# A tuned eight-core decoder kernel: the list order refined in a second pass, idle TensorE of the opening filled, and the last tile scaled by two engines

## The chip, the cores and the metric

The kernel runs on all 8 cores of one Trainium2 chip, one sample of the batch on each core. The metric is the time of the slowest core in microseconds (us). Profiles are taken on all cores of one execution; cores 0 to 3 are one die, 4 to 7 the other. A program on all cores has a second, slower state in some of its executions, in which cores of one die (or of both) run at a lower granted clock; times below are of fast runs unless it is said otherwise.

The engines are named TensorE (PE in the profile, its weight loads PEld), VectorE (DVE), ScalarE (ACT), GpSimd (POOL) and SyncE (SP, which only issues transfers here).

## The reference

A trunk of two layers, each with three sub-layers, on `x` of 8 samples x 2048 tokens x 1024 features:

```python
def modulate(x, g, mod):
    shift, scale, gate = jnp.split(mod, 3, axis=-1)
    h = rmsnorm(x, g) * (1.0 + scale[:, None, :]) + shift[:, None, :]
    return h, gate[:, None, :]

def swiglu(h, w_in, w_out):
    g, u = jnp.split(h @ w_in, 2, axis=-1)
    return (jax.nn.silu(g) * u) @ w_out

def reference(x, c, ...):
    c_act = jax.nn.silu(c)
    for l in range(DEPTH):                              # 2
        mod = c_act @ w_mod[l] + b_mod[l]               # (B, 9*D): one row of w_mod per number
        mod_f1, mod_mx, mod_f2 = jnp.split(mod, N_SUB, axis=-1)
        h, gate = modulate(x, norm_g[l, 0], mod_f1)
        x = x + 0.5 * gate * swiglu(h, w_ffn_in[l, 0], w_ffn_out[l, 0])
        h, gate = modulate(x, norm_g[l, 1], mod_mx)
        x = x + gate * mixer(h)                         # even l and odd l differ
        h, gate = modulate(x, norm_g[l, 2], mod_f2)
        x = x + 0.5 * gate * swiglu(h, w_ffn_in[l, 1], w_ffn_out[l, 1])
    return rmsnorm(x, final_g)
```

Two things matter here. Before the first matmul of the trunk can run, `h` needs the mean square of `x` and the numbers `shift` and `scale`, which are dot products of `c_act` with rows of `w_mod`. And all later sub-layers need further such rows, in the background.

## The kernel before

`x` lies in SBUF as 8 chunks of features (128 partitions) by 4 tiles of 512 tokens. The program is first recorded operation by operation by a greedy scheduler with a cost model, and then listed again: `relist` computes for each operation a due date backward from the greedy start times, and simulates the engines, each taking the ready operation with the earliest due date. The order that comes out is what each engine executes; at run time every engine follows its list strictly in order.

```python
    def relist(self, free=("dve", "act")):
        ...
        for o in ops:
            cost.append(o.end - o.start if o.semkey is None else o.issue)   # (two branches in the original)
            due.append(o.start + (0.0 if o.eng == "pe" else 8.0))
        ...                                   # due dates pulled forward along the dependencies
        while events:
            ...                               # each free engine takes the ready operation due first
    ...
    Sd.relist(("dve", "act", "pe"))           # once
```

Background work (row dots, squares) is recorded only while VectorE has little queued:

```python
    def slack():
        return Sd.tl["dve"].busy_after(Sd.tl["pe"].tail() - 0.5) < SLACK      # SLACK = 3

    def row_dma(q, where=None):               # load a row of wmod, 512 KB
        ...
        add("sp", I("dma_start", out=ap, in_=wmod_d[q]), writes=keys, cost=0.06, dma=dk, nbytes=128 * 4096)

    def row_dot(q):                           # its dot product, on VectorE
        ...
        stt(ap, ap, 1.0, CB[:], ALU.mult, ALU.mult, keys + ["CB"], [("MOD", 0, q)], n=1024, accum_out=MODT[:, q:q + 1])
```

In the opening 16 rows are needed. Four of them have their dot products on TensorE, as eight one-column fp32 matmuls each (the trace shows them as 16 instructions), the rest on VectorE. Fillers, matmuls whose result nobody reads, keep TensorE from idling; each has a fixed earliest time:

```python
    on_pe = (10, 12, 14, 15)
    ...
            if n in on_pe:
                for kc in range(NC):
                    add("pe", I("matmul", PS[b][:, 0:1], ap[:, kc * 128:(kc + 1) * 128], CT[:, kc:kc + 1], ...), ...)
            else:
                stt(ap, ap, 1.0, CB[:], ALU.mult, ALU.mult, keys + ["CB"], [("MOD", 0, q)], n=1024, accum_out=M)
    ...
    for n in range(WARM):                     # WARM = 36
        op = mm(PS[5][:], ONES[:], SQ[:, n % NSQ, :], True, True, [("SQ", n % NSQ), "ONES"], [("ps", 5)])
        op.after = 28.0 + n * 0.6
```

The last tile is scaled by VectorE in eight multiplies, stored two chunks at a time:

```python
                    rstd([3], True)           # 1/rms of the last tile: two activations, result in SBUF
                    for c in range(NC):
                        final_chunk(3, c)     # VectorE: X = X * g * rstd; a store after every second chunk
```

## Time and profile before

| | before |
|---|---|
| time, median of the first 3 runs | 1938.27 us (1936.89 to 1973.97; the longest is a slow run) |
| span of the profiled run, by core | 1927.7 to 1933.5 us |
| start of the 100th trunk matmul, mean of the cores | 86.6 us |
| from there to the last update of `x`, mean (least disturbed core) | 1831.7 us (1829.2) |
| from the last update to the end, mean | 12.1 us |

The last three rows cut the span at work, not at times, so that kernels can be compared although everything in them shifts: the **opening** up to the 100th matmul that reads a weight slot, the **body**, and the **tail**. They are worked out from each core's instruction records, and their sum is the core's span. The mean over the cores is of use for the opening and the tail. In the body the least disturbed core shows what the program itself takes. The lines of the profile that carry the argument are in the prediction.

### The profile page before, as it was taken

How to read it: one execution, taken by the hardware profiler on the slowest of the kernel's cores; microseconds unless marked ns; L12 is line 12 of the kernel's file. 1: busy time of each engine (PE TensorE's matmuls, PEld its weight loads, DVE VectorE, ACT ScalarE, POOL GpSimd, SP SyncE). 2: the span in 40 equal slices, each digit the busy share in tenths (PEclk: the TensorE clock that was granted, in tenths of full speed). 3: DMA queues.
4: the chain of work that ended last, by engine and by line, in shares of the span. 5: the costliest groups of instructions: out<-in, count | busy, mean ns of one | idle time of the engine just before them, and what ended most of it. 6: DMA issues, size and time to landing. Idle time of an engine off the chain costs nothing.

```text
span 1933.5 us, 25425 instructions; the slowest of 8 cores (1927.7 to 1933.5 us)
## 1 busy us (share of the span) xinstructions
PE 1880.4 (97%) x8706; PEld 853.4 (44%) x8706; DVE 1694.7 (88%) x3256; ACT 1030.3 (53%) x1738; POOL 174.6 (9%) x330
## 2 busy tenths in 40 slices
PE   3999999999999999999999999999999999999997
PEld 1544444444444444444444444444444444444443
DVE  4897999999988999999988888888998899898865
ACT  3444754456454564555456554654556655664343
POOL 0000000001212000000000000000000000000000
PEclk9899999999999999999999999999999999999999
DMA  9799568797676686867664554555453545445752
GB/s 278 147 174 218 92 119 184 177 190 155 169 177 157 143 190 148 168 137 158 148 119 81 89 87 83 89 96 88 77 88 66 87 77 94 78 74 87 175 86 95
DMA packets 67517, 248.72 MB, mean 129 GB/s; under 512 B 7616, under 2 KB 7744, under 8 KB 67136
## 3 DMA queue, kind: packets, MB, share of 16 engines
q0 software_dynamic: 42192, 153.64, 47.6%
q1 hardware_dynamic: 25200, 93.45, 15.1%
q8 instruction: 74, 1.21, 0.2%
q14 instruction: 51, 0.42, 0.1%
HBM read 392.29 MB, written 8.39 MB: 207 GB/s over the span
## 4 chain that ended last, share of the span: by engine, by line
PE 88%; DMA 4%; DVE 3%; ACT 2%; SPq 1%; issue 1%; POOL 0%; DVEq 0%
PE ps L465 88%; DMA WMOD<-wmod 3%; DMA SLOTS<-win 1%; SPq L465 1%; DVE WMOD L465 1%; DVE SLOTS L465 1%; DVE ACTB L465 1%; DVE TP L465 1%; DVE X L465 0%; ACT ps L465 0%; ACT PMH L465 0%; DVE ps L465 0%; ACT ACTB L465 0%; ACT TP L465 0%; ACT L465 0%
## 5 line engine op out<-in xcount | busy, mean ns | idle before, releaser
L465 PE MATMUL ps<-H,SLOTS 128*128 128x512 f16 x5440 | 1199.7, 379 | 9.3 <-ACT ps L465 3.3
L465 PEld LDWEIGHTS ps<-H,SLOTS 128*128 128x128 f16 x5440 | 530.1, 98 | 657.5 <-issue 28.3
L465 ACT ACTIVATE ps<-ps 128x512 f32<-128x512 f32 x684 | 397.0, 582 | 567.8 <-PE ps L465 529.1
L465 PE MATMUL ps<-ACTB,SLOTS 128*128 128x512 f16 x2780 | 613.8, 379 | 0.1
L465 PEld LDWEIGHTS ps<-ACTB,SLOTS 128*128 128x128 f16 x2780 | 271.8, 98 | 328.4 <-issue 1.4
L465 DVE TENSOR_TENSOR SLOTS<-SLOTS 128x512 f16<-128x512 f16 x996 | 395.0, 417 | 17.0 <-DMA SLOTS<-win 10.3
L465 DVE SCALAR_TENSOR_TENSOR X<-ps,GH,X 128x512 f32<-128x512 f32 x424 | 307.7, 743 | 38.0 <-PE ps L465 34.8
L465 ACT ACTIVATE TP<-ps 128x512 f32<-128x512 f32 x400 | 237.9, 595 | 129.2 <-PE ps L465 126.1
L465 DVE TENSOR_TENSOR ACTB<-TP,ps 128x512 f16<-128x512 f32 x368 | 248.6, 683 | 36.2 <-PE ps L465 22.7
L465 ACT ACTIVATE SQ<-X 128x512 bf16<-128x512 f32 x224 | 131.0, 622 | 111.3 <-DVE X L465 53.6
L465 POOL DMA_DIRECT2D SLOTS<-win x176 | 93.0, 530 | 1032.5 <-PE ps L465 957.8
L465 DVE TENSOR_TENSOR TP<-ps,TP 128x512 f32<-128x512 f32 x176 | 121.0, 687 | 52.4 <-ACT ps L465 50.8
L465 DVE SCALAR_TENSOR_TENSOR WMOD<-WMOD,CB 128x1024 f32<-128x1024 f32 x130 | 157.7, 1216 | 7.0 <-DMA WMOD<-wmod 6.9
L465 DVE TENSOR_TENSOR TP<-X,RS 128x512 f32<-128x512 f32 x192 | 128.8, 686 | 8.1 <-ACT ACTB L465 5.0
L465 DVE TENSOR_TENSOR ps<-ps,TP 128x512 f32<-128x512 f32 x176 | 122.3, 695 | 12.6 <-PE ps L465 10.9
L465 DVE TENSOR_TENSOR ACTB<-ACTB 128x1024 f16<-128x1024 f16 (+1 forms) x188 | 104.3, 565 | 1.4
L465 POOL DMA_DIRECT2D SLOTS<-wout x88 | 46.4, 528 | 502.2 <-PE ps L465 502.2
L465 PE MATMUL ps<-SQ,ONES 128*128 128x512 bf16 x166 | 56.6, 427 | 29.4 <-ACT SQ L465 24.3
L465 ACT ACTIVATE H<-TP,MODT,AS 128x512 f16<-128x512 f32 x81 | 62.5, 805 | 20.3 <-DVE TP L465 13.6
L465 ACT ACTIVATE PMH<-TP,MODT,AS 128x512 f16<-128x512 f32 x60 | 47.5, 805 | 18.9 <-DVE TP L465 18.7
L465 ACT ACTIVATE ACTB<-TP,MODT,AS 128x512 f16<-128x512 f32 x51 | 40.6, 808 | 13.2 <-PE ps L465 7.0
L465 DVE TENSOR_TENSOR SQ<-SQ 128x1024 bf16<-128x1024 bf16 (+1 forms) x56 | 36.2, 647 | 10.5 <-ACT SQ L465 10.1
(74 smaller groups left out, 539.1 us busy)
## 6 DMA issues: line engine op xcount, KB each, us to landing
SLOTS<-win POOLq DMA_DIRECT2D x176, 512.0 KB, 5.7
WMOD<-wmod SPq DMA_DIRECT2D x131, 512.0 KB, 5.9
SLOTS<-wout POOLq DMA_DIRECT2D x88, 512.0 KB, 5.4
SLOTS<-wab POOLq DMA_DIRECT2D x28, 512.0 KB, 8.7
outT<-X SPq DMA_DIRECT2D x16, 512.0 KB, 3.3
ACTB<-wmod SPq DMA_DIRECT2D x13, 512.0 KB, 28.6
X<-xT SPq DMA_DIRECT2D x2, 2048.0 KB, 22.1
X<-xT SPq DMA_DIRECT2D x8, 512.0 KB, 9.7
```

Source lines behind the costliest of these rows:

```text
L465: return lambda E: getattr(E, name)(*a, **k)
```

## The change

The intent, in three parts:

1. **Fillers wherever TensorE is idle.** Up to 150 instead of 36, without fixed times; the listing places one whenever TensorE has nothing else and cuts them off when the 21st TensorE operation after the opening is reached. The modelled transfer rate of the opening falls from 295 to 285 GB/s.
2. **Two passes of listing.** The second takes the start times of the first as its due dates. With it the slack for background work goes from 3 to 2.5.
3. **The last tile on two engines.** Five of its chunks on VectorE, reading the root from PSUM, three on GpSimd after ScalarE, stored from two queues; the squares of its last two chunks are no longer added in pairs.

```diff
-WARM = 36
+WARM = 150
+PASSES = 2
...
-            due.append(o.start + (0.0 if o.eng == "pe" else 8.0))
+            due.append(1e9 if o.filler else o.start + (0.0 if o.eng == "pe" else 8.0))
...
+        stop = [o.idx for o in ops if o.eng == "pe" and self.fill_to is not None and o.idx >= self.fill_to][20:21]
...
+                if x in stop:
+                    filling = False
+                if o.filler:
+                    o.filler = 1 if filling else 2
+                    cost[x] = o.issue if filling else 0.0
...
-    SLACK = 3
+    SLACK = 2.5
...
+    def final_part(t, a, b, eng):
+        for c in range(a, b):
+            if eng == "dve":
+                stt(Xv(c, t), Xv(c, t), SM[:, SM_FG + c:SM_FG + c + 1], PS[0][:], ALU.mult, ALU.mult, ...)
+            else:
+                act(Xv(c, t), Xv(c, t), AF.Copy, ..., scale=SM[:, SM_FG + c:SM_FG + c + 1])
+                add("pool", I("tensor_tensor", out=Xv(c, t), in0=Xv(c, t), in1=RS[:, t % 2, :], op=ALU.mult), ...)
+        add("sp" if eng == "dve" else "act", I("dma_start", ...), ...)
...
-    Sd.BW = 295e3
+    Sd.BW = 285e3
...
-        op = mm(PS[5][:], ONES[:], SQ[:, n % NSQ, :], True, True, ...)
-        op.after = 28.0 + n * 0.6
+        op = add("pe", I("matmul", PS[5][:], ONES[:], SQ[:, n % NSQ, :], ...), ..., cost=0.0)
+        op.issue, op.filler = c_pe(TT), 1
...
-                    rstd([3], True)
-                    for c in range(NC):
-                        final_chunk(3, c)
+                    rstd([3], True, load=(0.0, 0.0), bank=0)
+                    act(RS[:, 1, :], PS[0][:], AF.Copy, [("ps", 0)], [("RS", 1)])
+                    for a, b, eng in ((3, 5, "dve"), (0, 2, "pool"), (5, 7, "dve"), (2, 3, "pool"), (7, 8, "dve")):
+                        final_part(3, a, b, eng)
...
-    Sd.relist(("dve", "act", "pe"))
+    for _ in range(PASSES):
+        Sd.relist(("dve", "act", "pe"))
```

More of the change, by code (lines that the diff above doesn't have):

```diff
@@ L41 @@
     __slots__ = ("idx", "eng", "fn", "deps", "semkey", "start", "end", "pos", "seq", "signal",
-                 "dma_target", "waits", "clock", "issue", "nbytes", "bw", "after", "then", "gate")
+                 "dma_target", "waits", "clock", "issue", "nbytes", "bw", "after", "then", "gate", "filler")
 class Timeline:
@@ L92, in __init__ @@
         self.wire = Timeline(False)
+        self.fill_to = None
     def key_free(self, k):
@@ L155, in add @@
         op.gate = set()
+        op.filler = 0
         op.start = t
@@ L180, in relist @@
         for o in ops:
-            if o.semkey is None:
+            if o.semkey is None and not o.filler:
                 cost.append(o.end - o.start)
@@ L195, in relist @@
                 left[o.idx] += 1
+                if q.filler:
+                    continue
                 gap = cost[d] if q.semkey is None else cost[d] + 3.5 + q.nbytes / self.BW
@@ L217, in relist @@
         wire = Timeline(False)
+        filling = True
+        stop = [o.idx for o in ops if o.eng == "pe" and self.fill_to is not None and o.idx >= self.fill_to][20:21]
         while events:
@@ L270, in emit @@
         by_eng = {e: [] for e in self.ENGS}
-        order = sorted(ops, key=lambda o: (o.start, o.idx))
+        order = sorted((o for o in ops if o.filler < 2), key=lambda o: (o.start, o.idx))
+        live = max((o for o in order if o.filler), key=lambda o: o.start)
         for o in order:
@@ L290, in emit @@
                 q = ops[d]
+                if q.filler == 2:
+                    q = live
                 if q.semkey is not None:
@@ L904, in stats_evac, with rstd @@
         act(RS[:, t % 2, :], PS[st["b"]][:], AF.Copy, [("ps", st["b"])], [("RS", t % 2)])
-    def rstd(ts, direct=False, after=0.0, load=(1.3, 1.3)):
+    def rstd(ts, direct=False, after=0.0, load=(1.3, 1.3), bank=None):
         srcs = {}
@@ L925, in rstd @@
         for i, t in enumerate(ts):
-            chain.append(add("act", I("activation", out=RS[:, t % 2, :], in_=RS[:, t % 2, :], func=AF.Exp, scale=-0.5),
-                             reads=[("RS", t % 2)], writes=[("RS", t % 2)], cost=0.75 + (load[1] if i == n - 1 else 0.0), after=at))
+            out, key = (RS[:, t % 2, :], ("RS", t % 2)) if bank is None else (PS[bank][:], ("ps", bank))
+            chain.append(add("act", I("activation", out=out, in_=RS[:, t % 2, :], func=AF.Exp, scale=-0.5),
+                             reads=[("RS", t % 2)], writes=[key], cost=0.75 + (load[1] if i == n - 1 else 0.0), after=at))
         chain[0].gate = set(table_ops)
@@ L1166, in part @@
                     self.w.done(dch // 2)
-                if self.last and dch % 2 == 1:
+                if self.last and n >= len(self.units) - 2:
+                    while self.sq:
+                        self.sq.pop(0)[0]()
+                    z = sq_rot.next()
+                    act(SQ[:, z, :], Xv(dch, 2 * self.p + tt), AF.Square, [Xk(dch, 2 * self.p + tt)], [("SQ", z)], src="sb")
+                    ones_mm(z, 2 * self.p + tt, NC // 2 + 1)
+                elif self.last and dch % 2 == 1:
                     self.flush_ones(NSQ // 2 - 1)
-                    self.sq.append((squares(dch - 1, 2 * self.p + tt, 2), 2 * self.p + tt))
+                    (q, at), t = squares(dch - 1, 2 * self.p + tt, 2), 2 * self.p + tt
+                    self.sq.append((lambda z=q[0], t=t: ones_mm(z, t, NC // 2 + tt), at))
         def flush_ones(self, most=NSQ // 2):
-            while self.sq and (len(self.sq) > most or self.sq[0][0][1] <= Sd.tl["pe"].tail()):
-                (q, _), t = self.sq.pop(0)
-                ones_mm(q[0], t)
+            while self.sq and (len(self.sq) > most or self.sq[0][1] <= Sd.tl["pe"].tail()):
+                self.sq.pop(0)[0]()
         def segments(self, tail):
@@ L1279, in final_chunk @@
                 reads=[Xk(c - 1, t), Xk(c, t)], writes=[("OUT", t, c)], cost=0.06, dma=("OUT", t, c), nbytes=128 * 4096)
+    def final_part(t, a, b, eng):
+        for c in range(a, b):
+            if eng == "dve":
+                stt(Xv(c, t), Xv(c, t), SM[:, SM_FG + c:SM_FG + c + 1], PS[0][:], ALU.mult, ALU.mult,
+                    [Xk(c, t), "SM", ("ps", 0)], [Xk(c, t)])
+            else:
+                act(Xv(c, t), Xv(c, t), AF.Copy, [Xk(c, t), "SM"], [Xk(c, t)], src="sb", scale=SM[:, SM_FG + c:SM_FG + c + 1])
+                add("pool", I("tensor_tensor", out=Xv(c, t), in0=Xv(c, t), in1=RS[:, t % 2, :], op=ALU.mult),
+                    reads=[Xk(c, t), ("RS", t % 2)], writes=[Xk(c, t)], cost=c_pool(TT))
+        add("sp" if eng == "dve" else "act", I("dma_start", out=outT[t][:, a * TT:b * TT], in_=X[:, t, a:b, :]),
+            reads=[Xk(c, t) for c in range(a, b)], writes=[("OUT", t, c) for c in range(a, b)], cost=0.06, dma=("OUT", t, a),
+            nbytes=128 * 2048 * (b - a))
     BS = Af32[:, 40 * 256:42 * 256]
@@ L1575, in build_nc @@
     for n in range(WARM):
-        op = mm(PS[5][:], ONES[:], SQ[:, n % NSQ, :], True, True, [("SQ", n % NSQ), "ONES"], [("ps", 5)])
-        op.after = 28.0 + n * 0.6
-        op.start, op.end = op.after, op.after + op.issue
+        op = add("pe", I("matmul", PS[5][:], ONES[:], SQ[:, n % NSQ, :], start=True, stop=True, skip_group_check=True),
+                 reads=[("SQ", n % NSQ), "ONES"], writes=[("ps", 5)], cost=0.0)
+        op.issue, op.filler = c_pe(TT), 1
     tmp_rot.items = list(range(NTP))
@@ L1603, in build_nc @@
     Sd.BW = Sched.BW
+    Sd.fill_to = len(Sd.ops)
     for ph in PHASES:
@@ L1722, in build_nc @@
                         final_chunk(2, c)
-                    while dn.sq:
-                        (q, _), t = dn.sq.pop(0)
-                        ones_mm(q[0], t)
-                    rstd([3], True)
-                    for c in range(NC):
-                        final_chunk(3, c)
+                    rstd([3], True, load=(0.0, 0.0), bank=0)
+                    act(RS[:, 1, :], PS[0][:], AF.Copy, [("ps", 0)], [("RS", 1)])
+                    for a, b, eng in ((3, 5, "dve"), (0, 2, "pool"), (5, 7, "dve"), (2, 3, "pool"), (7, 8, "dve")):
+                        final_part(3, a, b, eng)
         else:
@@ L1738, in build_nc @@
         marks.append((sub, p, t_begin, Sd.tl["pe"].tail()))
-    add("sp", None, reads=[("OUT", t, c) for t in range(4) for c in (1, 3, 5, 7)], cost=0.01)
-    Sd.relist(("dve", "act", "pe"))
+    add("sp", None, reads=[("OUT", t, c) for t in range(4) for c in ((1, 3, 5, 7) if t < 3 else range(NC))], cost=0.01)
+    for _ in range(PASSES):
+        Sd.relist(("dve", "act", "pe"))
     with nc.Block() as block:
```

## The prediction

> **What bounds the kernel now.** I read the page's engine rows first, then the table of windows, the waits of TensorE, the chain of waits, and last the timelines of the opening and of the last tile.
>
> ```profile
> PE 1880.4 (97%) x8706; PEld 853.4 (44%) x8706; DVE 1694.7 (88%) x3256; ACT 1030.3 (53%) x1738; POOL 174.6 (9%) x330
> PE 88%; DMA 4%; DVE 3%; ACT 2%; SPq 1%; issue 1%; POOL 0%; DVEq 0%
> 1000.00:1200.00 200.00, 199.01 (x923) 89.91 (x921) 168.90 (x321) 108.08 (x184) 16.89 (x32) 1.00 0.51 87
> ```
>
> TensorE is the bound, and the bound is hard: in the steady stage (third line: a stretch of 200 us, busy TensorE, count in brackets) 923 matmuls in 199.0 us of busy time are 0.2156 us each at granted clock 1.00. The change removes no matmul of the trunk, so only time in which TensorE is not at this rate can be won. Two windows over the body say how much that is:
>
> ```profile
> 72.00:1400.00 1328.00, 1320.06 (x6151) 597.10 (x6149) 1209.47 (x2329) 716.95 (x1219) 131.49 (x245) 1.00 0.67 137
> 1400.00:1921.00 521.00, 518.78 (x2399) 233.89 (x2397) 441.99 (x815) 280.24 (x470) 39.59 (x75) 1.00 0.49 89
> ```
>
> 1328.0 - 1320.1 = 7.9 us and 521.0 - 518.8 = 2.2 us: in 1849 us of body TensorE is idle for only **10.1 us** on the slowest core. (On the seven other cores the first number is 3.1 to 7.2 us.) About 4 us of it lie between 154 and 212 us, where the DMA share reaches 1.00. The rest is 0.2 to 1 us at a time. Outside the body there are the opening (0 to 72 us) and the tail (1921 to 1933.5 us).
>
> ```profile
> 46.00:48.00 2.00, 0.00 (x0) 0.00 (x0) 2.00 (x5) 0.66 (x1) 0.00 (x0) 1.00 1.00 274
> 48.00:50.00 2.00, 1.91 (x9) 1.76 (x10) 2.00 (x5) 2.00 (x4) 0.00 (x0) 0.52 1.03 221
> ...
> 60.00:62.00 2.00, 2.00 (x11) 1.92 (x11) 0.28 (x2) 0.00 (x0) 0.32 (x1) 0.50 0.95 277
> 62.00:64.00 2.00, 2.00 (x6) 0.71 (x5) 2.00 (x6) 0.81 (x1) 0.00 (x0) 0.50 1.05 119
> ```
>
> The last three columns are granted clock, DMA share and GB/s. TensorE stood still for 3.1 us before 48.1 us (it waited for a row of wmod), and from there to about 65 us it ran at half clock, although it was busy. That is the stretch that matters in the chain:
>
> ```profile
> 26.36 27.54 DMA WMOD<-wmod
> 54.03 10.51 PE ps L465 x42
> 65.06 1.51 ACT H L465 x2
> 66.60 1.21 DVE H L465 x4
> 69.48 83.97 PE ps L465 x388
> ```
>
> The opening is first a transfer (the row lands at 53.9 us, DMA engines full), then 10.5 us of cold TensorE, then 4.9 us of ScalarE and VectorE that finish h, then dense matmuls from 69.5 us.
>
> **What the Trainium skill says.** "TensorE: Matmul & The Clock Gate", Part 1, "What's actually happening": the half-rate clock is the idle default, about 3.4 us of sustained work lifts it and an idle window of that length brings it back. The trace agrees on the fall (3.1 us idle, then 0.52), but not plainly on the rise: TensorE's row is full from 54 to 62 us and the clock stays at 0.50. Most of those instructions are one-column fp32 matmuls, so a busy row is not enough; denser 512-column fillers should be. "DMA: Bandwidth & Descriptors", "Issuing engines are not separate DMA queues": transfers from several issuers share the same 16 engines; a second issuer saves only issue time. The trace shows the consequence in the tail (below). "GPSIMD Engine Reference", 3.1: a two-input fp32 tensor_tensor of 2048 columns takes 4497 ns against 2293 on VectorE; no run here has this operation on GpSimd. "SBUF — State Buffer", "Who interferes with whom": a VectorE instruction with two SBUF inputs blocks a GpSimd one that reads SBUF; with one it does not. The new VectorE multiply reads one input from PSUM, so I expect no blocking; the trace before has no such pair.
>
> **Part 1, fillers.** The 36 fillers at fixed times become up to 150, placed by the lister wherever TensorE would be idle, and cut off after the first 20 trunk operations. They need the second tile's squares (done at 37.6 us). From there to 62 us are 24.4 us; four rows of 16 one-column matmuls take some 8.2 us warm (64 x 0.129, from the row at 42.4 to 44.5 us: 16 in 2.06). The other 16 us hold some 75 fillers of 0.216 us, so 150 suffice. Gain, step by step:
> - The row that lands at 53.9 us: its 16 small matmuls with five fillers in between took 54.03 to 58.40 = 4.37 us, and the next row's 16 took 3.55 us. Warm and without fillers between: 2 x 2.06 = 4.1 us. Saved: 7.9 - 4.1 = **3.8 us**.
> - The first 20 trunk matmuls ran from 62.19 to 69.12 us with gaps, against 20 x 0.216 = 4.3 us: 2.6 us more could come. But the chain after the last row also has VectorE (0.2 + 1.3), ScalarE (2.2) and VectorE (1.5), about 5 us for the last parts of h, and sums of weights at 0.42 us each compete for VectorE. I count **1.5 us**.
> - The transfer that lands at 53.9 us is not touched. Sum: about -5 us, from -2 to -7.
> Some is given back. From 80 to 190 us the DMA share is 0.81 to 1.03, and waits for wmod rows and X of the third and fourth tile end TensorE's 3.4 us of gaps from 170 to 190. Starting 5 us earlier meets the same transfers earlier; I put +1 us on it.
>
> **Part 2, second pass of listing.** No instruction is added. The second pass takes the start times of the first list as due dates instead of those of the greedy one; with the lower slack (2.5 for 3) it moves VectorE's background work. It can win at most the 10.1 us above and can lose as much, since it reorders 8,700 matmuls by a model's times. Waits that come from slot or transfer timing stay. I choose a third: **-3 us**, from -7 to +3.
>
> **Part 3, the last tile.** Now: last trunk matmul ends at about 1920.8, first two chunks scaled at 1926.0, and then:
>
> ```profile
> 1926.00:1927.00 1.00, 0.00 (x0) 0.00 (x0) 1.00 (x3) 0.00 (x0) 0.00 (x0) 0.50 0.12 49
> 1927.00:1928.00 1.00, 0.00 (x0) 0.00 (x0) 1.00 (x3) 0.00 (x0) 0.00 (x0) 0.50 0.97 393
> ...
> 1931.00:1932.00 1.00, 0.00 (x0) 0.00 (x0) 0.00 (x0) 0.00 (x0) 0.00 (x0) 0.50 0.99 401
> 1932.00:1933.00 1.00, 0.00 (x0) 0.00 (x0) 0.00 (x0) 0.00 (x0) 0.00 (x0) 0.50 0.22 86
> ```
>
> The store of 2 MB runs at 0.97 to 0.99 of the DMA engines from about 1926.9 to 1932.2 us, 5.3 us without a gap. So the tail is bound by when the first pair of chunks is ready, plus the transfer, not by VectorE's eight multiplies (5.4 us).
> - Removed: the add of two squares on the path, 1922.22 to the matmul at 1922.79 = -0.57 us. One more ones matmul, 0.22 us, lies beside other work.
> - Added: the root now goes to PSUM bank 0, and ScalarE copies it back to RS for GpSimd. The scheduler treats a PSUM read as exclusive, so VectorE's first multiply waits for that copy: +0.6 us (an ACTIVATE of this shape is 582 ns). The multiplies also wait for one another, 0.77 us instead of 0.67: +0.2 us for the first pair.
> - VectorE does five chunks (3.9 us), GpSimd three: an estimate from the page's 4497 ns for 2048 columns, 1.2 us each, 3.6 us in all. Both end before the store could drain.
> Sum: -0.57 + 0.6 + 0.2 = **+0.2 us**, from -1 to +1.5.
>
> **The rivals.** (a) The opening is transfer-bound to the end: warm TensorE would then wait for h or for slots, the gain is 1 us, and the total is near 1934. For it: share 0.9 to 1.06 until 58 us. Against: after 53.9 us the chain names TensorE, not a DMA. (b) Fillers stand in the way: TensorE takes them in the listed order, so where data lands earlier than the model assumed (285 GB/s instead of 295 now), real work queues behind fillers at 0.216 us each; 10 too many cost 2 us. Or the model is early, the fillers run out, and the clock falls again before 54 us: then part 1 gives nothing. (c) The second pass is much better than I give it: all 10 us of idle go, and the total is near 1922. For it: VectorE is at 88%, so its order is what keeps TensorE waiting. Against: the waits are already short and no cause repeats. (d) The new order adds bubbles where VectorE is full (62.2 of 63 us from 212 to 275): the total is near 1938. I see no rival of 2%, or 39 us: the body is 1849 us with 10 us idle, and opening and tail give 10 us between them at the very best.
>
> **Range and chances.** Base: the fast runs, 1938.3 and 1936.9, mean 1937.6 (1974.0 is a slow one). -5 + 1 - 3 + 0.2 = -6.8, which gives 1930.8; I lean towards (c) by 1 us, because the pass was chosen by someone who measured. The range spans the better ends of parts 1 and 2 without give-back (about -15) and a plain zero: 1922 to 1937. Faster by over 2% would need 1899 and slower 1976: 1 in 100 each.
>
> **What would show it.** Right: granted clock near 1.00 from 38 to 66 us; the two last rows of wmod in about 4 us of TensorE; dense matmuls from about 64.5 us; idle TensorE in the body about 7 us, still with a group between 154 and 212; a store of the last tile at about 0.99 for 5.3 us, from the last trunk matmul to the end 12.5 to 13 us as now. Wrong: a clock that falls to 0.50 again before 54 us, row matmuls that queue behind fillers, idle time in the body under 3 or over 12 us, a store that starts more than 1 us earlier or later behind the last matmul, or GpSimd multiplies of 2 us and over, which would make the last piece late.

## The result, and the profile after

The changed kernel took 1931.17 us (median of 4 runs, 1929.68 to 1935.55, all fast); the kernel before, in the same rounds, 1937.67 (median of 4 runs, of which one was slow; 1937.07 is the median of the three fast ones). The ratio is 0.9972, with a 95% interval of 0.9951 to 0.9992. Ratios here are the mean time of one kernel's fast runs over that of the other's of the same rounds, so they are not quite the ratio of the medians quoted beside them. The total lies 1.4 us from the predicted 1929.8. Its parts do not:

| mean of the 8 cores, us | before | after | difference | predicted |
|---|---|---|---|---|
| opening (to the 100th trunk matmul) | 86.6 | 87.2 | +0.6 | -5 |
| body (to the last update of `x`) | 1831.7 | 1825.4 | -6.3 | -3, and +1 given back |
| body, least disturbed core | 1829.2 | 1823.6 | -5.6 | |
| tail (to the end) | 12.1 | 12.6 | +0.4 | +0.2 |

The sum of the differences of the means, +0.6 - 6.3 + 0.4 = -5.3, is the difference of the mean spans, 1930.5 and 1925.2. So the opening, on which most of the gain was placed, gave nothing (its cores lie between 85.4 and 89.0 us, so +0.6 is no clear loss either), and the body gave twice what was placed on the second pass.

The page of the changed kernel (engines, chain) and two windows of the body of its slowest core, 7. Columns of a window: its start and end, length, then busy time and count of TensorE, weight loads, VectorE, ScalarE and GpSimd, then granted clock, DMA share, GB/s.

```profile
PE 1883.1 (98%) x8722; PEld 855.1 (44%) x8722; DVE 1692.6 (88%) x3252; ACT 1030.2 (53%) x1742; POOL 175.9 (9%) x333
...
PE 93%; DMA 4%; SPq 1%; DVE 1%; ACT 0%; issue 0%; POOL 0%
...
72.00:1400.00 1328.00, 1323.78 (x6173) 599.55 (x6172) 1210.93 (x2333) 716.96 (x1224) 129.03 (x245) 1.00 0.67 138
1400.00:1905.00 505.00, 505.00 (x2341) 228.90 (x2340) 431.66 (x796) 276.86 (x464) 39.59 (x75) 1.00 0.50 88
```

In the body TensorE is now idle for 1328.0 - 1323.8 = 4.2 us on the slowest core, and for none at all after 1400 us. The chain names TensorE for 93% instead of 88%. On this core nothing is left to win after 1400 us.

The opening is another picture. The first block is TensorE's timeline (start, duration, what it did, in brackets what it waited for before), the second VectorE's, the third shows windows of the same stretch, all of the slowest core:

```profile
54.12 3.54 PE L480 MATMUL ps<-CT,WMOD 128*128 128x1 f32 x16 [0.32 <-DMA WMOD<-wmod]
57.52 3.55 PE L480 MATMUL ps<-CT,ACTB 128*128 128x1 f32 x16
60.94 3.15 PE L480 MATMUL ps<-SQ,ONES 128*128 128x512 bf16 x7
63.88 2.94 PE L480 MATMUL ps<-H,SLOTS 128*128 128x512 f16 x8
```

```profile
57.70 0.16 DVE L480 TENSOR_TENSOR MODT<-ps,SM 128x1 f32<-128x1 f32 x1 [2.64 <-PE ps L480]
...
61.11 0.22 DVE L480 SCALAR_TENSOR_TENSOR AS<-ps,SB,SM 128x1 f32<-128x1 f32 x1 [1.32 <-PE ps L480]
```

```profile
52.00:56.00 4.00, 3.68 (x14) 2.25 (x13) 3.06 (x7) 0.00 (x0) 0.00 (x0) 0.50 1.04 295
56.00:60.00 4.00, 4.00 (x20) 4.00 (x20) 2.09 (x5) 0.78 (x2) 1.05 (x2) 0.50 0.62 103
60.00:64.00 4.00, 4.00 (x14) 2.07 (x14) 2.89 (x9) 2.96 (x5) 0.00 (x0) 0.50 0.98 213
```

The clock is at 0.50 again (first number of the last three columns), although TensorE is busy; the two last rows take 3.54 and 3.55 us, as the cold one before did, and not the predicted 4.1 us for both. VectorE, which needs their results, waits 2.64 and 1.32 us for TensorE. Of the 150 fillers the listing kept 51, and 37 of them had run when the second to last row was taken up at 54.12 us. (Of the seven matmuls at 60.94 us five are fillers; two, in the kernel before as well, write the banks of the rows once more.)

The slowest core is not the whole picture. This is core 0 of the same execution, where the clock was at 1.00 from 55.6 to 59.0 us:

```profile
55.12 2.06 PE L480 MATMUL ps<-CT,WMOD 128*128 128x1 f32 x16
57.04 1.93 PE L480 MATMUL ps<-CT,ACTB 128*128 128x1 f32 x16
```

Here the two rows take 2.06 + 1.93 = 3.99 us, as predicted, and still the 100th trunk matmul starts at 85.4 us, only 1.2 us before the mean of the kernel before. Core 0 alone was warm through both rows; cores 3, 5 and 7 were cold through both, the other four warm for a part. The tail is shown with its experiments.

### The profile page after: what moved, and what is told of

Its sections match the earlier page's. It is cut to its first block, busy times and chain, and to the rows that moved or that the text cites. A ratio compares the mean times of both kernels' runs of the same rounds, so it can differ in the third digit from the quotient of the medians.

```text
span 1928.1 us, 25440 instructions; the slowest of 8 cores (1921.6 to 1928.1 us)
## 1 busy us (share of the span) xinstructions
PE 1883.1 (98%) x8722; PEld 855.1 (44%) x8722; DVE 1692.6 (88%) x3252; ACT 1030.2 (53%) x1742; POOL 175.9 (9%) x333
## 4 chain that ended last, share of the span: by engine, by line
PE 93%; DMA 4%; SPq 1%; DVE 1%; ACT 0%; issue 0%; POOL 0%
PE ps L480 93%; DMA WMOD<-wmod 3%; SPq L480 1%; DMA SLOTS<-win 1%; DMA ACTB<-wmod 0%; DVE X L480 0%; DVE ACTB L480 0%; DVE WMOD L480 0%; ACT PMH L480 0%; ACT ps L480 0%; ACT ACTB L480 0%; ACT RS L480 0%; ACT L480 0%; DVE TP L480 0%; ACT TP L480 0%
## 5 line engine op out<-in xcount | busy, mean ns | idle before, releaser
L480 DVE TENSOR_TENSOR H<-H 128x1024 f16<-128x1024 f16 (+1 forms) x72 | 43.2, 623 | 2.1 <-ACT H L480 2.1
```

Of the source, the lines that this page charges most:

```text
L480: return lambda E: getattr(E, name)(*a, **k)
```

## The experiments

Twelve kernels ran. The text ahead of each states the theories that it was to tell apart.

### One part of the change undone at a time

**Change with one pass of listing.**

```diff
-PASSES = 2
+PASSES = 1
```

> The changed kernel with one pass of listing instead of two; fillers, slack 2.5 and the new tail stay. Theory P (the second pass carries the gain: idle TensorE in the body, 72 to 1905 us, fell from a mean of 7.7 us over the cores to 2.9): the idle time goes back to 6 to 9 us and the time to about 1936 to 1938, ratio to before 0.999 to 1.001. Rival S (the lower slack and the other greedy list carry it): idle stays at 3 to 4 us, ratio about 0.997. Rival F (fillers carry it): ratio about 0.997 and the opening the same as in the changed kernel, with the body's idle near 3 us.

Measured: 1954.65 and 1956.31 us, the two others slow (2109.20 and 2281.10). In the profiled run cores 6 and 7 ran at a granted clock of 0.81 for some 140 us from about 65 us on (383 matmuls between 100 and 200 us, where the undisturbed core 0 does 463). The run was counted as fast, since this is two cores of a die of four, but it says nothing of the change. The other six cores are undisturbed: their spans are 1923.0 to 1928.8 us, and the body takes 1825.7 us on the least disturbed one, 2.1 us more than with two passes.

**The kernel before with two passes.**

```diff
-    Sd.relist(("dve", "act", "pe"))
+    for _ in range(2):
+        Sd.relist(("dve", "act", "pe"))
```

> The kernel before with the listing run twice and nothing else changed. Theory P: idle TensorE in the body falls from 7.7 to 2 to 4 us on the mean of the cores, and the time by 4 to 6 us, ratio 0.997 to 0.998. Rivals S and F: idle stays at 6 to 9 us, ratio 0.999 to 1.001.

Measured: 1938.83, 1959.54 and 1959.68 us, a fourth run slow (2022.66); ratio 1.0072 (0.9994 to 1.0149). Two of these three, the profiled one among them, are disturbed in the same way (in the profiled run cores 0 and 1, for 160 us from about 70 us on), so the time decides nothing. On the other six cores the body takes 1829.3 us at the least, against 1829.2 before: in the body the second pass **alone** gives nothing.

**Change with the old fillers.** WARM back to 36, each with its fixed earliest time.

```diff
-WARM = 150
+WARM = 36
...
+        op.after = 28.0 + n * 0.6
```

> The changed kernel with the 36 fillers at fixed times of the kernel before. The 100th trunk matmul starts at 87.2 us on the mean of the cores in the changed kernel and at 86.6 before. Theory Q (the new fillers give nothing and cost under 1 us): the 100th comes at 86 to 87 us and the whole time is the same as the changed kernel's or up to 1 us less. Rival F (the fillers are worth what was predicted, about 4 us, and something else ate it): the 100th comes at 89 to 92 us and the time rises by 3 to 5 us.

Measured: 1933.04 us (1931.25 to 1934.82), ratio 0.9970 (0.9953 to 0.9988), beside 0.9972 for the whole change. The opening takes 86.8 us against 87.2 with the new fillers; its cores lie between 85.3 and 88.3 us, so these two do not differ. The new fillers gave nothing.

**Change with the old last tile.** Old squares, eight multiplies on VectorE, four stores of two chunks.

```diff
-                    rstd([3], True, load=(0.0, 0.0), bank=0)
-                    act(RS[:, 1, :], PS[0][:], AF.Copy, [("ps", 0)], [("RS", 1)])
-                    for a, b, eng in (...):
-                        final_part(3, a, b, eng)
+                    rstd([3], True)
+                    for c in range(NC):
+                        final_chunk(3, c)
```

> The changed kernel with the last tile scaled as before, by VectorE alone from SBUF and with the squares of the last two units added first. From the last trunk matmul to the end were 12.9 us before and 13.35 us in the changed kernel, on the mean of the cores. Theory T (the store of 2 MB at a full DMA share sets the tail, and the copy back to SBUF costs more than the shorter root saves): 12.9 us again, the whole time 0.3 to 0.5 us less. Rival: the tail becomes 13.8 us or more, because the five multiplies beside GpSimd do help and something else lengthened the tail.

Measured: fast runs 1932.28 and 1934.93 us (two others slow), ratio 0.9973 (0.9949 to 0.9997). Mean times from the end of the last trunk matmul, in us:

| | first pair scaled | last VectorE multiply ends | first packet | last packet | end |
|---|---|---|---|---|---|
| before | 5.27 | 9.24 | 6.16 | 12.10 | 12.92 |
| changed kernel, old last tile | 5.27 | 9.24 | 6.16 | 12.62 | 13.35 |
| changed kernel | 5.52 | 7.87 | 6.42 | 12.62 | 13.35 |

The multiplies end 1.4 us earlier and the end does not move. With the old tile in the changed kernel the end is as late as with the new one; neither theory's number (12.9, or 13.8 and more) came. So nothing shows that the +0.4 us against the kernel before is the new tile's. The end varies from run to run: with the same new tile it comes 12.64 to 13.37 us after the last trunk matmul in the profiled runs. The timeline of the changed kernel's last tile, and two windows of its store:

```profile
1918.87 3.88 DVE L480 SCALAR_TENSOR_TENSOR X<-X,SM,ps 128x512 f32<-128x512 f32 x5 [3.20 <-ACT RS L480]
1918.92 3.71 POOL L480 TENSOR_TENSOR X<-X,RS 128x512 f32<-128x512 f32 x3 [41.83 <-ACT RS L480]
```

```profile
1922.00:1924.00 2.00, 0.00 (x0) 0.00 (x0) 0.75 (x1) 0.00 (x0) 0.63 (x1) 0.50 1.00 393
1924.00:1926.00 2.00, 0.00 (x0) 0.00 (x0) 0.00 (x0) 0.00 (x0) 0.00 (x0) 0.50 1.01 389
```

GpSimd took 3.71 / 3 = 1.24 us for each multiply, beside VectorE's 0.78, and neither shows a wait for the other. The multiplies are over at about 1922.8 us; after them only the store is left, 2.1 MB in all, at a DMA share of 1.0.

### Which number carries the body

**The kernel before with the lower slack only.**

```diff
-    SLACK = 3
+    SLACK = 2.5
```

> The kernel before with the slack for background work at 2.5 instead of 3 and nothing else changed: one pass, old fillers, old tail. The last runs showed that the stretch from the 32nd update of X to the last one takes 1667.0 us before, 1662.9 in the changed kernel, 1663.1 with one pass, and 1668.1 with two passes on the kernel before. Theory S (the slack, through the greedy list, carries that part): 1662 to 1664 us here, and the stretch from the 224th to the 320th update 397.8 us instead of 400.0. Rival (something else that the changed kernels share, such as the modelled bandwidth of the opening): 1666 to 1668 us, and 399.7 to 400.0.

Measured: 1934.97 us (median of the three fast runs, 1934.36 to 1935.08; one was slow), ratio 0.9988 (0.9968 to 1.0008). Its body takes 1825.5 us on the least disturbed core. With the two runs above this gives a square of four (body, least disturbed core, us):

| | one pass | two passes |
|---|---|---|
| slack 3 | 1829.2 (before) | 1829.3 (before, two passes) |
| slack 2.5 | 1825.5 (before, lower slack); 1825.7 (change, one pass) | 1823.6 (the change) |

The lower slack gives 3.7 us, the second pass 2 us more, but only on top of it. How far such a number can be trusted, the other runs tell: seven more kernels share slack, passes and unpaced loads with the change; in six of them the least disturbed core takes 1823.3 to 1823.7 us, in one 1824.5. Two windows of core 3 show where the gain lies. In both this core was undisturbed in all four runs (in the kernel before it had lost some 4 us earlier, to the wait of the next section). First the kernel before, then the kernel before with two passes, then with the lower slack, then the change:

```profile
600.00:800.00 200.00, 199.90 (x938) 90.79 (x937) 189.93 (x352) 108.28 (x182) 16.45 (x31) 1.00 0.73 161
...
1400.00:1460.00 60.00, 58.77 (x271) 25.98 (x270) 58.11 (x114) 33.15 (x62) 4.22 (x8) 1.00 0.49 85
```

```profile
600.00:800.00 200.00, 198.05 (x916) 89.06 (x914) 187.31 (x350) 106.80 (x181) 15.85 (x30) 1.00 0.72 158
...
1400.00:1460.00 60.00, 58.46 (x271) 26.05 (x269) 57.25 (x112) 33.61 (x62) 4.75 (x9) 1.00 0.46 74
```

```profile
600.00:800.00 200.00, 198.61 (x919) 89.43 (x918) 185.07 (x348) 106.59 (x182) 15.83 (x30) 1.00 0.70 153
...
1400.00:1460.00 60.00, 60.00 (x280) 27.20 (x279) 57.77 (x112) 33.66 (x61) 4.76 (x9) 1.00 0.48 80
```

```profile
600.00:800.00 200.00, 199.90 (x938) 90.58 (x936) 185.75 (x350) 108.08 (x182) 16.36 (x31) 1.00 0.71 153
...
1400.00:1460.00 60.00, 60.00 (x280) 27.19 (x279) 58.09 (x111) 33.01 (x61) 4.76 (x9) 1.00 0.47 81
```

Busy TensorE in the second window is 58.8, 58.5, 60.0 and 60.0 us: 1.2 us of waiting that the lower slack removes and the second pass does not touch. Waits of about 0.9 us between 900 and 1000 us and between 1650 and 1700 us go in the same way. In the first window it is 199.9, 198.1, 198.6 and 199.9: each of the two alone brings in new waits of 1.3 to 1.9 us, and together they do not. In the time of the slowest core less of the 3.7 us is seen, since in the profiled run core 7 lost 94.1 - 85.1 = 9.0 us to the wait of the next section.

A trap is worth telling. When I first cut the body into stretches between updates of `x`, the stretch from the 16th to the 32nd update was 2 us shorter in the change than in the change with one pass, and I put this down to a removed wait. A count of its matmuls showed 376 instead of 384: eight of them, 8 x 0.2156 = 1.7 us of work, had only moved over the border. A stretch is comparable only if its work is the same.

### The wait that picks the slowest core

In all kernels with the usual loads, some cores lose up to 10 us between 154 and 215 us (their stretch from the 16th to the 32nd update is up to 92.9 us long, where the same kernel's shortest is 83.1), others nothing, and which ones differs from run to run. In the profiled run of the change with the old last tile it was core 2, and core 5 showed no such wait. The chain of waits of core 2 (start, duration, what), and a window after it:

```profile
155.70 12.60 DMA WMOD<-wmod
...
170.04 19.39 DMA WMOD<-wmod
...
191.32 0.69 DVE ACTB L480
...
193.36 1.86 PE ps L480 x4
```

```profile
195.00:200.00 5.00, 4.78 (x14) 1.88 (x14) 1.76 (x4) 2.25 (x4) 0.00 (x0) 0.56 0.10 38
```

Two rows of wmod, asked for at 155.7 and 170.0 us for the phase after, took 12.6 and 19.4 us to land, in a stretch with a DMA share of 0.94 to 1.06. VectorE takes its list in order and stood at the dot product of such a row; TensorE then waited for what VectorE should have delivered, and after the wait ran at clock 0.56 for 5 us. To test this, loads of rows were delayed:

**Change with paced row loads.** Each load of a row after the opening also waits for the last matmul listed before it.

```diff
-        add("sp", I("dma_start", out=ap, in_=wmod_d[q]), ...)
+        op = add("sp", I("dma_start", out=ap, in_=wmod_d[q]), ..., after=Sd.tl["pe"].tail() ...)
+        if Sd.fill_to is not None:
+            op.deps.add(max(o.idx for o in Sd.ops[-120:] if o.eng == "pe"))
```

> The changed kernel in which each load of a row of wmod after the opening also waits for the matmul that was listed last when the row was asked for. So no row is loaded between 125 and 255 us, where the DMA share is about 1.0. Theory W (a row dot of a later phase, taken early, blocks VectorE until its late row lands, and this random wait of 0 to 9 us on each core sets the slowest core): the stretch from the 16th to the 32nd update is 83.0 to 83.6 us on every core instead of 83.1 to 86.1 (83.1 to 92.0 in the run with the old tail), the cores' spans lie within 3 us, and the slowest is 1923 to 1926, 3 to 6 us less. Rival (X of the third and fourth tile or the weights are what is late): the stretch stays spread over 83 to 90 us and the time is the same or worse.

Measured: fast runs 1939.84 and 1941.13 us (two others slow), ratio 1.0018 (0.9998 to 1.0038). The stretch from the 16th to the 32nd update took 82.6 to 83.3 us on **all** eight cores, with 374 matmuls in it where the change has 376, so the loads were the cause of the random wait. (A DMA share of about 1.0, which the expectation puts on 125 to 255 us, the traces show only from about 155 to 195 us; from 215 us on it is 0.5 to 0.6.) But now rows came late around 480 us (core 3 waits for one from 473.7 to 485.0): on the mean of the cores TensorE idles for 7.8 us between 400 and 600 us, in the changed kernel for 0.1. The cure cost more than the disease.

### What held the opening

**Change with the four opening rows on VectorE.**

```diff
-    on_pe = (10, 12, 14, 15)
+    on_pe = ()
```

The four rows are then also loaded from the array that the other rows come from, 512 KB each as before.

> The changed kernel in which the four rows of the opening that TensorE multiplied by one-column matmuls go to VectorE like the others, so that only 512-column fillers run on TensorE from 37 to 59 us. Theory C (one-column fp32 matmuls do not hold the clock, even beside fillers, so the fillers could not do their work): granted clock 1.00 from 42 us to the first trunk matmuls on all cores, and the 100th trunk matmul at 83 to 86 us instead of 87.2. Rival (the fillers themselves do not hold the clock, or waits do not let them): the clock falls to 0.50 between 47 and 66 us again. If the clock stays up but the 100th trunk matmul comes at 87 us or later, the cold clock was not what the opening waits for.

Measured: 1927.74 us (1926.34 to 1931.02), ratio **0.9955** (0.9939 to 0.9970). The opening takes 82.4 us against 87.2. TensorE's timeline and one window of core 7, then VectorE's dot product of the last row:

```profile
34.86 22.13 PE L480 MATMUL ps<-SQ,ONES 128*128 128x512 bf16 x91 [5.70 <-ACT SQ L480]
56.82 1.67 PE L480 MATMUL ps<-H,SLOTS 128*128 128x512 f16 x7
```

```profile
56.00:60.00 4.00, 4.00 (x20) 1.82 (x19) 3.92 (x8) 1.15 (x2) 0.00 (x0) 1.00 0.06 14
```

```profile
57.23 1.22 DVE L480 SCALAR_TENSOR_TENSOR WMOD<-WMOD,CB 128x1024 f32<-128x1024 f32 x1
```

Fillers now run without a break, the clock stays at 1.00, and the trunk begins at 56.8 instead of 63.9 us. The last dot product ends at 57.23 + 1.22 = 58.5 us; in the changed kernel VectorE had the last sum from TensorE only at 61.1 us. Not all of the gain is VectorE's wait. ScalarE makes three parts of `h` from the last sums; first core 7 of the changed kernel, then of this run:

```profile
61.49 2.22 ACT L480 ACTIVATE H<-TP,MODT,AS 128x512 f16<-128x512 f32 x3 [0.75 <-DVE AS L480]
```

```profile
61.61 2.21 ACT L480 ACTIVATE H<-TP,MODT,AS 128x512 f16<-128x512 f32 x3
```

They end at 63.7 and 63.8 us, no earlier here. But TensorE, which in the changed kernel had the two rows and those seven matmuls to do from 54.1 to 63.9 us, has run its first trunk matmuls by then. How much each of the two paths gives was not separated. This run alone also leaves open whether it is the row dots or the warm clock. The next ones bear on that.

**Change with the fillers cut off at the first trunk operation.**

```diff
-        stop = [...][20:21]
+        stop = [...][0:1]
```

> The changed kernel with fillers cut at the first trunk matmul instead of the 21st: 42 fillers instead of 51, none behind the first trunk matmul (nine now). Theory B (fillers queue in front of trunk matmuls): the 100th trunk matmul comes 1 to 2 us sooner, 85.2 to 86.2 us on the mean of the cores, and the time falls by 1 to 2 us. Rival (the trunk waits there for h and for sums on VectorE, and the fillers only fill those waits): 87 us again, with idle TensorE of about 2 us between 60 and 72 us.

Measured: 1932.99 us (median of the three fast runs, 1931.22 to 1935.15; one was slow), ratio 0.9980 (0.9964 to 0.9997). The opening takes 86.3 us, 1.0 us less than in the change, which fits the cost of nine fillers between the first trunk matmuls; as the cores lie between 84.3 and 88.0 us the size is rough, and the whole time did not fall.

**Rows on VectorE and one filler instead of 150.**

```diff
-WARM = 150
+WARM = 1
...
-    on_pe = (10, 12, 14, 15)
+    on_pe = ()
```

> The kernel of the run with all opening rows on VectorE, but with one filler instead of up to 150. Theory C (the gain of that run, the 100th trunk matmul at 82.4 us instead of 87.2, needs both: no one-column matmuls and fillers that hold the clock): the clock is 0.50 from about 40 us to at least 60 us, and the 100th trunk matmul comes at 84 to 86 us. Rival D (only the shorter chain of VectorE against TensorE's row dots matters): the 100th trunk matmul at 82 to 83 us as with fillers, although the clock is low.

Measured: fast runs 1924.44 and 1926.70 us, two others slow (2070.58 and 2153.43), and no ratio. The opening takes 81.3 us, 1.1 us less than with fillers, on all cores (80.7 to 81.7), although the clock is at 0.50 from about 42 to 63 us. So without row dots on TensorE the cold clock does not hold the trunk: the opening is the shortest of all. Fillers and warm clock together cost 1.1 us here rather than gaining any.

With row dots on TensorE the clock did count, and traces at hand show it. The changed kernel, the one with the old last tile and the one with the last tile on VectorE alone (below) have the same opening, 24 cores in all. On the 3 cores where the last two rows ran warm, in 3.9 us, the 100th trunk matmul starts at 85.1 us in the mean; on the 11 where both ran cold, in 7.1 us, at 88.2. By this comparison of cores (it is no experiment) a clock that held would have given some 3 us over a cold core, 1.5 us over the kernel before (86.6). Row dots on VectorE (82.4 with fillers, 81.3 without) give 2.7 to 3.8 us beyond that.

### The last tile, and the parts together

**Change with the last tile on VectorE alone, its first chunk stored alone.** The direct squares of the last chunks stay.

```diff
-                    for a, b, eng in ((3, 5, "dve"), (0, 2, "pool"), (5, 7, "dve"), (2, 3, "pool"), (7, 8, "dve")):
-                        final_part(3, a, b, eng)
+                    for a, b in ((0, 1), (1, 3), (3, 5), (5, 7), (7, 8)):
+                        for c in range(a, b):
+                            stt(Xv(c, 3), Xv(c, 3), SM[:, SM_FG + c:SM_FG + c + 1], RS[:, 1, :], ...)
+                        add("sp", I("dma_start", out=outT[3][:, a * TT:b * TT], in_=X[:, 3, a:b, :]), ...)
```

> The changed kernel with another last tile: VectorE alone, from SBUF (no copy of the root, no GpSimd), the squares of the last two units still straight to TensorE, and the first chunk stored by itself before pairs. Theory T (the last 2 MB leave at the full DMA share, so the tail is the time to the first store plus about 6 us, whoever multiplies): VectorE's last multiply ends at 8.6 to 8.8 us after the last trunk matmul, later than the 7.87 of the changed kernel, and still the first packet comes at 4.8 to 5.0 us instead of 6.42 and the end at 11.6 to 12.1 instead of 13.35. Rival (the multiplies set it): the end at 13.5 us or later.

Measured: 1933.70 us (median of the three fast runs, 1932.09 to 1935.52; one was slow), ratio 0.9982 (0.9964 to 0.9999): by time no difference that the random wait would not hide. From the last trunk matmul the first packet leaves after 5.04 us instead of 6.42, and the end comes after 12.44 instead of 13.35 us, with the multiplies finished 0.9 us **later** (8.78 us). So the multiplies do not set the end. The end is later than expected (11.6 to 12.1), and only 0.2 us below the earliest one of the new tile in other runs (12.64).

**Rows on VectorE, row loads paced in the first two phases only, this last tile.**

> All that helped together: the changed kernel with the opening rows on VectorE, each wmod row load of the first two phases waiting for the matmul listed last when it was asked for, and the last tile as in the tail run. Expected from the parts: 4.8 us from the opening (another 0.5 to 1.5 from rows that no longer load inside it), no random wait between the 16th and 32nd update (82.6 to 83.4 us on every core), 1.3 us from the tail. Slowest core about 1915 to 1919, ratio to before 0.989 to 0.991. Where pacing only moves the wait to the phase after (as it did over all phases, 433 to 439 us from the 32nd to the 128th update instead of 423), the ratio is 0.993 or worse.

Measured: fast runs 1963.98 to 1965.71 us, the three others slow (1966.03, 2240.78, 2241.73); ratio 1.0141 (1.0123 to 1.0160): a miss. Runs counted as fast are disturbed too. In the profiled one cores 2, 3, 6 and 7 had spans of 1958.0 to 1961.8 us, the others 1927.0 to 1933.9. Windows of core 6:

```profile
480.00:489.00 9.00, 6.73 (x21) 2.68 (x22) 4.71 (x9) 6.45 (x11) 0.69 (x2) 0.62 1.02 218
...
500.00:600.00 100.00, 100.00 (x407) 42.67 (x405) 69.23 (x113) 43.45 (x74) 5.89 (x11) 0.81 0.60 131
```

Late rows left gaps up to 489 us, the clock fell, and from there to about 651 us these four cores were granted 0.81 of the full clock: 407 matmuls between 500 and 600 us, where core 6 of the changed kernel does 489 at clock 1.00. 162 us at 0.81 instead of 1.00 lose 162 x 0.19 = 31 us; the two groups of cores differ in the mean by 29 us. That it began just after the gap in all four is measured; the other four cores had gaps too and kept their clock. Why it began there, on these cores, stays open.

**The parts that had proved themselves, without pacing.** Rows on VectorE, one filler, this last tile; two passes and slack 2.5 as in the change.

> A version that should beat both: the changed kernel with the four opening rows of wmod on VectorE, one filler instead of up to 150, and the last tile scaled by VectorE alone with its first chunk stored alone. Theory D (the row dots on TensorE delayed the trunk; neither the fillers nor the clock before 62 us mattered): the 100th trunk matmul starts at 81 to 82 us as in the run without row dots and fillers, the tail from the last trunk matmul to the end is 12.0 to 12.6 us as in the run with the first chunk stored alone, and the slowest core comes to 1921 to 1928 us, a ratio to the kernel before of 0.991 to 0.996. Rival (the random wait between 154 and 215 us sets the slowest core whatever comes before it): the slowest core stays at 1928 to 1932 us, 0.996 to 0.998, with one core that has 5 us and more of idle TensorE in that stretch. If the opening without fillers leaves TensorE at half clock beyond 65 us, the 100th trunk matmul is after 83 us.

Measured: **1926.70 us** median (5 of 6 runs 1926.49 to 1928.27, one slow), against 1937.57 of the kernel before; ratio **0.9948** (0.9933 to 0.9962). It beats the kernel before. The change stood at 0.9972 in other rounds; the two intervals overlap by 0.0011, the fast runs (1929.68 to 1935.55 there) do not. The last tile adds nothing that is seen in the time: without it (rows on VectorE and one filler) the fast runs took 1924.44 and 1926.70 us. The opening takes 81.3 us, the mean span is 1921.2 us. From the last trunk matmul to the end it takes 12.8 us, a little above the 12.0 to 12.6 expected. The slowest core is picked by the random wait again: core 4 took 90.9 us from the 16th to the 32nd update, where core 3 took 83.2. Its opening, and the row it waited for at 162 us:

```profile
55.44 2.29 PE L480 MATMUL ps<-H,SLOTS 128*128 128x512 f16 x5 [10.87 <-DVE SLOTS L480]
59.26 12.91 PE L480 MATMUL ps<-H,SLOTS 128*128 128x512 f16 x48 [1.53 <-DVE H L480]
```

```profile
161.81 20.38 DMA WMOD<-wmod
```

TensorE idles for 10.87 us before 55.4, runs its first 20 trunk matmuls cold, and is nevertheless 6 us ahead of the changed kernel by the 100th. The wait behind that load cost core 4 some 90.9 - 83.2 = 7.7 us; it is the largest single item left on the slowest core.

## Why the prediction was right or wrong

The total was right and two of its three terms were not; their errors cancelled, which was luck.

- **What bounds the kernel** was right: TensorE at 0.2156 us a matmul in the body; everything won was idle time or an end of the program.
- **Part 1, -5 us and +1 given back: wrong; +0.6 measured.** The step that failed is "Warm and without fillers between: 2 x 2.06 = 4.1 us". On the slowest core the rows took 3.54 + 3.55 us on a cold TensorE. Its clock had fallen at 48.9 us, after TensorE had stood for 1.40 us before a row that was listed ahead of further fillers and had not landed; the eight fillers from 50.2 to 53.8 us did not bring the clock back. This is the second half of rival (b), "the clock falls again before 54 us: then part 1 gives nothing", which was given no share of the sum. Where the clock did hold, on core 0, the size was right (3.99 us), but the 100th trunk matmul was only 1.2 us earlier than before, and the seven matmuls listed between the last row and the trunk, five of them fillers, took 3.0 us. Beneath it lies a choice that the prediction never questioned: the rows were left on TensorE. Off it, without fillers and at half clock, the opening is 5.9 us shorter than in the change, and 3.8 us shorter than on its warm cores. The second term, 1.5 us from gaps between the first 20 trunk matmuls, ran the other way: nine fillers stood in those gaps, and cutting them off gained about 1 us.
- **Part 2, -3 us: the size was off, and its owner.** Measured -5.6 us on the least disturbed core and -6.3 in the mean. The prediction gave the gain to the second pass and named the slack beside it. The slack alone gives 3.7 us, the pass 2 us more, and without the lower slack nothing. The statement that waits "that come from slot or transfer timing stay" was right: the random wait of up to 10 us stayed in every kernel whose row loads were not delayed.
- **Part 3, +0.2 us: right at the start of the store,** +0.26 us; the end is unmoved against the old tile in the changed kernel, and +0.4 us against the kernel before within what runs differ by. GpSimd's 1.24 us met the estimate of 1.2. The trace shows no wait of VectorE and GpSimd for each other, which agrees with what the prediction took from "SBUF — State Buffer", "Who interferes with whom".
- **Signs named ahead.** Idle TensorE in the body "about 7 us": 4.2 on the slowest core, which is inside the bounds of 3 and 12 us. Clock near 1.00 from 38 to 66 us: no, 0.50 on the slowest core from 49 to 66 us, and below 1.00 for some of it on every core. Dense matmuls from 64.5 us: no, from 70.3 us on the slowest core. Store at 0.99: yes.

What stays open: how the gain of moving the rows divides between VectorE's wait and TensorE's own list, why VectorE's order with either measure alone brings new waits at 600 to 800 us, and why the granted clock fell to 0.81 on some cores for 138 to 162 us in the profiled runs of three kernels.

## What to carry to other kernels

Before an engine is kept warm for a piece of work, ask whether that work should be there at all: four dot products of 1.2 us on VectorE beat the same ones at 2 to 3.5 us on TensorE. Both engines take their lists in order, so all that was listed behind the rows waited too. And look at more than the slowest core: here cores of one execution differed in their clock, and that difference measured what the clock was worth. Change one parameter at a time even where a change looks like one idea; here a single number that looked like a detail carried most of the gain. Lastly, cut a trace at equal work, with its count checked, before calling one stretch shorter than another.

## What the Trainium skill lacked or had wrong

- "TensorE: Matmul & The Clock Gate", "What's actually happening": it says that about 3.4 us of sustained work lift the clock. On the slowest core of the changed kernel a TensorE busy with one-column fp32 matmuls from 54.1 to 60.9 us stayed at 0.50; on core 0 it stood at 1.00 from 55.6 to 59.0 us, when TensorE had next to nothing but such matmuls, and then at 0.50 for the next 3.4 us. 91 fillers of 512 columns kept it at 1.00 (rows on VectorE). The page has no word on which work counts as busy.
- The same page, "Seeing it yourself": it advises to budget 1.95 GHz, 13/16 of the clock, for dense matmuls on all cores, and says that the whole die is taken there. Here all eight cores ran dense for over 1800 us at a granted clock of 1.00 in most runs. In the slow runs a whole die did run low, as the page says: in one (2321.11 us) the means of cores 0 to 3 were 0.81 to 0.82. But in fast runs a clock of 0.81 appeared on two cores of a die at a time (6 and 7; 0 and 1; 2, 3, 6 and 7), for 138 to 162 us, and then ended under the same load.
- The same page, "Back-to-back issue gap": it gives about 131 ns as the sustained spacing of 512-column matmuls and says that the formula for a single one, 216 ns, over-counts. In the steady stage of the kernel before it is 199.0 us / 923 = 215.6 ns, the figure of the formula, which the page elsewhere also gives as measured.
- "GPSIMD Engine Reference", 3.1: for a `tensor_tensor` in fp32 only 2048 columns are given as measured (4497 ns). 512 columns took 1.24 us, against 1.12 for a quarter of it.
- No page that I read warns of an early prefetch on an engine's ordered list: rows that landed after 12.6 and 19.4 us at a DMA share near 1.0 held VectorE and with it TensorE, up to 10 us on some cores and nothing on others.
